# First layer's experts: state-space work queued behind the activation, the output gate folded into the last group, shorter root and norm chains

## The chip, the cores and the metric

The kernel runs on one core of a Trainium2 chip. The time is the device time of one execution in microseconds (us); less is better. For the kernel before there are three runs and one profiled execution, which is a run of its own.

## The reference, cut to what matters

A two-layer backbone over 512 tokens (256 of context, 256 latent) of width 1024. Every layer normalises the stream with a modulated RMSNorm, mixes, adds a gated residual, and then runs a mixture of experts over a second modulated norm. The first layer treats context and latent tokens alike in shape, but with modulation rows of their own (`cg2` and `g2` below); the second layer's experts see the latent tokens alone.

```python
f = hier_moe(jnp.concatenate([modnorm(xc, norm_g[i, 1], csh2, csc2),
                              modnorm(x, norm_g[i, 1], sh2, sc2)], axis=1), *moe_p)
xc = xc + cg2 * f[:, :n_ctx]
x = x + g2 * f[:, n_ctx:]
...
def rmsnorm(t, g):
    tf = t.astype(F32)
    y = tf * lax.rsqrt(jnp.mean(tf * tf, axis=-1, keepdims=True) + EPS)
    return (y * g.astype(F32)).astype(t.dtype)
...
hid = jax.nn.silu(t @ w_gate[e]) * (t @ w_up[e])
y = y + gates[:, e:e + 1] * (hid @ w_down[e])
```

There are 32 experts, each token goes to two of them. All arithmetic is float32.

## The kernel before, in words

The stream X stands in four tiles of 128 tokens by 1024 (tiles 0 and 1 context, 2 and 3 latent). In `tail` a layer's experts are worked off in groups: 13 in the first layer, 11 in the second. A group holds two or four experts that share the 128 rows of one tile of gathered tokens, 64 or 32 rows each. `pair` does one group:

- the gate and up products into one PSUM bank (tag g, L242), with weight tiles of 1 MB from a ring of buffers that SP loads in order (L1592);
- the next group's gathered rows are transposed on PE and copied (`pair_rows`, `then`);
- SiLU on ScalarE (L1748), the product with the up half on VectorE (L1749);
- two transposes of the hidden tile, a copy (`cp`, L254 on VectorE or L256 on ScalarE; without an engine's name the two take turns), and the down products into two banks (tag m);
- each half of y, times the token's gate, is split in a rounded part (ScalarE, L1772) and the rest (VectorE, L1773);
- a 0/1 matrix S takes the rows back to token order, tile by tile (tag c), and VectorE adds each 128x512 result to a sum F (L1786).

In the last group `add` takes the place of the sum in F: in the first layer it multiplies by the gate row and adds to X (L1553, L1554; three of the eight additions go to GpSimd). The sums F of the earlier groups are multiplied by the gate row and added to X by `gated` (L1542, L1543), two tiles before the last group's SiLU (`work`) and two behind its product L1749 (`after`). In the second layer's last group the gate row is already multiplied into the halves (`cols`, L1768 to L1770), and `add` is one addition (L1551).

Beside the first layer's groups 2 to 12 runs `s5_prepare`, a generator of 67 steps: small vector work, zeroing copies, two passes of products for the second layer's state-space operators (`prod`, L1147 to L1155), PE transposes and small products. `pair` calls it six steps at a time, `self.work(work)`, in front of SiLU.

The second layer begins with `norm1`: the squares of each tile on ScalarE (L436), a root for a pair of tiles on VectorE (`rsqrt_`, L174 to L185, ten dependent steps on a column or a few), the scaling of both tiles (L453, 128x1024 each), then transposes on PE (L246, four to a bank) and evictions with scale and shift (L469, L471). The first layer's `norm1`, near the start of the kernel, is the same with plain copies, and stands among the modulation products, whose weight tiles are loaded four ahead. `rsqrt_` also serves the tail's tiles (one column), the heads (ten columns), the filter (four) and the final norm (two).

The order of the instructions on each engine is fixed when the program is built: a scheduler takes the instructions in the order of writing, as they become ready by its own estimates. `issue_after(ins)` queues what its block writes for the engine of `ins` behind `ins`, on that engine alone. The lines are those of the profile.

Of the kernel before, what the change touches and what calls it, by code (L numbers as in the profile page):

```python
# [21 lines left out]
P = 128  # L22
# [8 lines left out]
SHARE = ((0, 0), (1, 0), (2, 0))  # L31
# [130 lines left out]

def small(pool, name, n):

    return pool.tile([P, 10], F32, name=name, tag=name)[:, :n]


def rsqrt_(nc, pool, src, n, scale, src2=None):


    V = nc.vector
    x, y, t, q = (small(pool, "rs" + c, n) for c in "xytq")
    if src2 is None:
        V.tensor_scalar(x, src, float(scale), EPS, op0=ALU.mult, op1=ALU.add)  # L174
    else:
        V.scalar_tensor_tensor(x, src, EPS, src2, op0=ALU.add, op1=ALU.add)
    V.tensor_scalar(y.bitcast(I32), x.bitcast(I32), -0.5, float(0x5F375C00), op0=ALU.mult, op1=ALU.add)
    V.scalar_tensor_tensor(t, y, -0.5, y, op0=ALU.mult, op1=ALU.mult)
    V.tensor_mul(t, t, x)
    V.scalar_tensor_tensor(y, t, 1.5009, y, op0=ALU.add, op1=ALU.mult)  # L180
    V.tensor_mul(t, y, y)
    V.tensor_mul(t, t, x)
    V.tensor_scalar(q, t, 0.375, -1.25, op0=ALU.mult, op1=ALU.add)
    V.tensor_mul(q, q, t)
    V.scalar_tensor_tensor(y, q, 1.875, y, op0=ALU.add, op1=ALU.mult)  # L185
    return y
# [44 lines left out]
class Body:  # L231
# [193 lines left out]
    def rms(self, tiles, tmp):  # L425

        n = len(tiles)
        if n == 1:
            ss = small(self.sm, "ss", 2)
            for h in range(2):  # L430
                cs = slice(512 * h, 512 * h + 512)
                self.nc.scalar.activation(tmp[0], self.X[tiles[0]][:, cs], AF.Square, scale=1.0 / 32, accum_out=ss[:, h:h + 1])
            return rsqrt_(self.nc, self.sm, ss[:, 0:1], 1, 1.0, ss[:, 1:2])
        ss = small(self.sm, "ss", n)
        for j, i in enumerate(tiles):
            self.nc.scalar.activation(tmp[j], self.X[i][:], AF.Square, accum_out=ss[:, j:j + 1])  # L436
        return rsqrt_(self.nc, self.sm, ss, n, 1.0 / D)

    def norm1(self, layer):
# [9 lines left out]
        for b in range(2):  # L449
            xn = [next(ring) for _ in range(2)]  # L450
            r = self.rms([2 * b, 2 * b + 1], xn)
            for i in range(2):
                nc.vector.tensor_scalar(xn[i], self.X[2 * b + i][:], r[:, i:i + 1], None, op0=ALU.mult)  # L453
            for j in range(4):
# [3 lines left out]
                for k in range(4):  # L458
                    d, i = 2 * j + k // 2, k % 2
                    self.tr(ps[:, 128 * k:128 * k + 128], xn[i][:, 128 * d:128 * d + 128])  # L460
# [895 lines left out]
    def tail(self, layer, tiles, mix, mixT):  # L1356
# [5 lines left out]
        with ExitStack() as es:  # L1362
# [164 lines left out]
            for q in range(nG):  # L1527
# [9 lines left out]
                gate2 = lambda t: row(g2, 0 if local else t // 2)  # L1537
                if q == nG - 1:
# [9 lines left out]
                    def add(n, cs, ps):  # L1548
                        t = tiles[n]
                        if local:  # L1550
                            V.tensor_add(self.X[t][:, cs], self.X[t][:, cs], ps)  # L1551
                            return
                        V.tensor_mul(F[n][:, cs], gate2(t)[:, cs], ps)  # L1553
                        (nc.gpsimd if (n, cs.start) in SHARE else V).tensor_add(self.X[t][:, cs], self.X[t][:, cs], F[n][:, cs])  # L1554
# [5 lines left out]
                               (row(g2, 0), row(g2, 1)) if local and final else None, q == 0 and not local)  # L1560
# [170 lines left out]
    def pair(self, q, xT, T, part, n, tokc, gate, F, work=0, after=0, then=None, cols=None, new=False):  # L1731
# [15 lines left out]
        self.work(work)  # L1747
        nc.scalar.activation(hid, ps[:, :256], AF.Silu)  # L1748
        m = V.tensor_mul(hid, hid, ps[:, 256:])  # L1749
        if after:  # L1750
            with self.tc.issue_after(m.ins):
                self.work(after)
# [3 lines left out]
        self.cp(hidT, ps[:, :256].rearrange("p (k t) -> p k t", t=128))  # L1756
# [49 lines left out]
    def final(self):  # L1806
# [4 lines left out]
        for t in (2, 3):  # L1811
            u = self.unit()
            y.append(u.f[:, :D])
            for h in range(2):
                nc.scalar.activation(u.f[:, D:D + 512], self.X[t][:, 512 * h:512 * h + 512], AF.Square, scale=1.0 / 32, accum_out=ss[:, k:k + 1])
                k += 1
# [226 lines left out]
```

## Time and profile before

| | us |
|---|---|
| median of 3 runs | 1200.01 (1198.22 to 1200.25) |
| the profiled execution's own time | 1194.71 |
| its span, first to last instruction | 1192.7 |
| PE busy | 1087.7 |
| VectorE busy | 699.0 |
| ScalarE busy | 319.2 |
| read from HBM and written | 298.82 MB, mean 251 GB/s |

Times in rows are in us from the span's start. PE is the matrix engine, PEld its weight loads, DVE is VectorE, ACT ScalarE, POOL GpSimd, SP the queue that issues most loads. A name such as psg is the PSUM tile of tag g. A group of rows gives busy time, count and mean; the chain of waits gives the pieces of work that the end depended on, in order of time. A matrix product of float32 is recorded as two PE instructions, a transpose as one.

### The profile page before, as it was taken

What the parts mean: (1) busy time and instruction counts of PE and PEld (TensorE: products, weight loads), DVE (VectorE), ACT (ScalarE), POOL (GpSimd) and SP (SyncE); (2) the same over time, 40 slices, a digit from 0 to 9 for tenths busy, and PEclk for the clock granted to TensorE, in tenths of its full rate; (3) what the DMA queues carried; (4) which work ended last, traced back from release to release, by engine and by line L of the source; (5) the groups of instructions that cost most, each with busy time, mean ns of one, the idle gap of its engine ahead of it and who ended that gap; (6) DMA issues with size and microseconds to landing.
All of it is one profiled execution on the core that took longest, in us unless ns stands there. A gap on an engine that the chain in (4) does not pass through costs nothing.

```text
span 1192.7 us, 17395 instructions
## 1 busy us (share of the span) xinstructions
PE 1087.7 (91%) x6528; PEld 560.3 (47%) x6528; DVE 699.0 (59%) x1915; ACT 319.2 (27%) x651; POOL 52.6 (4%) x64
## 2 busy tenths in 40 slices
PE   5999999999998899989989879999989899999975
PEld 2356556544456333334435246556665554444331
DVE  4876889558567375363453678857564554433324
ACT  3323212135123211120221065245442221212111
POOL 0001410000000100000000100010000000000000
PEclk9999999959999899999999889999989899999998
DMA  8777533640404589999798512345637285999994
GB/s 306 283 266 265 212 131 129 239 196 4 173 36 135 206 349 419 421 419 413 294 421 320 208 36 75 121 137 201 231 137 292 83 342 229 422 421 421 420 420 190
DMA packets 48601, 298.82 MB, mean 251 GB/s; under 512 B 6407, under 2 KB 8984, under 8 KB 15165
## 3 DMA queue, kind: packets, MB, share of 16 engines
q1 hardware_dynamic: 40380, 281.58, 60.4%
q10 hardware_dynamic: 5728, 11.86, 2.7%
q0 software_dynamic: 2400, 4.19, 1.0%
q8 instruction: 54, 0.88, 0.3%
q14 instruction: 39, 0.31, 0.1%
HBM read 295.68 MB, written 4.26 MB: 251 GB/s over the span
## 4 chain that ended last, share of the span: by engine, by line
PE 45%; DVE 10%; DMA 9%; ACT 2%; issue 1%; DVEq 0%; SPq 0%; ACTq 0%
PE psg L242 15%; PE psm L242 13%; PE psc L242 11%; DMA big<-w_e 9%; PE pst L242 3%; PE pst L246 2%; DVE big L1280 1%; PE psc L825 1%; DVE big L1216 1%; DVE big L1147 1%; DVE fr L1773 1%; ACT fr L1772 0%; DVE big L254 0%; ACT big L1155 0%; DVE big L1212 0%
## 5 line engine op out<-in xcount | busy, mean ns | idle before, releaser
L242 PE MATMUL psm<-big 128*128 128x512 f32 (+8 forms) x672 | 197.7, 466 | 4.6 <-ACT big L256 2.4
L242 PE MATMUL psg<-big,big 128*32 128x512 f32 (+1 forms) x720 | 176.6, 618 | 9.6 <-DMA big<-w_e 9.6
L242 PE MATMUL psm<-big,big 128*32 128x64 f32 (+7 forms) x600 | 129.2, 446 | 8.0 <-DVE big L254 4.1
L242 PEld LDWEIGHTS psm<-big 128*128 128x128 f32 (+2 forms) x672 | 91.3, 166 | 87.8 <-issue 64.7
L242 PE MATMUL psc<-big 128*32 128x32 f32 (+8 forms) x1108 | 111.6, 268 | 17.3 <-ACT big L514 7.8
L242 PE MATMUL psg<-big 128*64 128x512 f32 (+1 forms) x264 | 95.6, 617 | 8.1 <-PEq L1621 6.7
L242 PEld LDWEIGHTS psc<-big 128*32 128x32 f32 (+3 forms) x1108 | 73.7, 128 | 56.2 <-issue 29.7
L242 PE MATMUL psc<-fr 128*128 128x512 f32 x296 | 94.0, 431 | 4.1 <-DVE fr L1773 3.1
L1786 DVE TENSOR_TENSOR big<-big,psc 128x512 f32<-128x512 f32 x128 | 82.6, 684 | 22.0 <-PE psc L242 21.5
L246 PE MATMUL pst<-k_par,big 128*128 128x128 f32 (+2 forms) x470 | 80.5, 299 | 15.8 <-DVE big L453 3.7
L246 PEld LDWEIGHTS pst<-k_par,big 128*128 128x128 f32 (+2 forms) x470 | 55.8, 149 | 68.0 <-issue 30.1
L242 PEld LDWEIGHTS psc<-fr 128*128 128x128 f32 x296 | 49.5, 187 | 76.8 <-DVE big L1786 20.3
L242 PEld LDWEIGHTS psg<-big,big 128*32 128x32 f32 (+1 forms) x720 | 44.2, 124 | 86.2 <-issue 69.8
L242 PEld LDWEIGHTS psm<-big,big 128*32 128x32 f32 (+2 forms) x600 | 54.0, 145 | 51.8 <-issue 39.2
L1773 DVE SCALAR_TENSOR_TENSOR fr<-psm,tab,fr 128x512 fp32r<-128x512 f32 x46 | 34.6, 751 | 74.1 <-ACT fr L1772 71.7
L256 ACT ACTIVATE big<-pst 128x512 f32<-128x512 f32 (+2 forms) x88 | 47.3, 547 | 92.2 <-PE pst L246 85.0
L242 PE MATMUL psm<-parts 128*128 128x512 f32 x264 | 67.8, 405 | 0.5 <-DVE parts L651 0.5
L242 PE MATMUL psm<-big,bm 128*64 128x512 f32 (+1 forms) x256 | 56.4, 644 | 9.7 <-DVE bm L254 6.0
L242 PEld LDWEIGHTS psm<-parts 128*128 128x128 f32 x264 | 48.1, 188 | 19.0 <-issue 7.2
L1772 ACT ACTIVATE fr<-psm,tab 128x512 fp32r<-128x512 f32 x46 | 31.6, 687 | 70.9 <-PE psm L242 70.9
L242 PEld LDWEIGHTS psg<-big 128*64 128x64 f32 (+1 forms) x264 | 25.1, 131 | 48.5 <-issue 45.7
L1749 DVE TENSOR_TENSOR big<-big,psg 128x256 f32<-128x256 f32 x11 | 4.6, 420 | 72.3 <-ACT big L1748 72.3
(399 smaller groups left out, 1379.5 us busy)
## 6 DMA issues: line engine op xcount, KB each, us to landing
big<-w_e SPq DMA_DIRECT2D x187, 1024.0 KB, 15.8
big<-w_mod SPq DMA_DIRECT2D x36, 1024.0 KB, 5.1
x<-w_mod SPq DMA_DIRECT2D x12, 1024.0 KB, 4.9
big<-w_out SPq DMA_DIRECT2D x8, 1024.0 KB, 6.7
big<-w_hy SPq DMA_DIRECT2D x6, 1024.0 KB, 6.0
big<-modd ACTq DMA_DIRECT2D x10, 512.0 KB, 10.9
x<-w_e SPq DMA_DIRECT2D x5, 1024.0 KB, 13.6
h2d<-big ACTq DMA_DIRECT2D x6, 512.0 KB, 4.5
```

What stands on the lines that cost most here:

```text
L242: self.product = self.nc.tensor.matmul(out, lhsT, rhs, start=start, stop=stop)
L246: return self.nc.tensor.transpose(out, in_, self.ident[:k, :k])
L256: self.nc.scalar.activation(out, in_, AF.Copy)
L825: m = self.nc.tensor.matmul(ps[:, :k.shape[-1]], q, k, start=True, stop=True)
L1147: V.tensor_mul(sc[:, j, :].rearrange("p (d u v h) -> p d u v h", d=2, u=4, v=4), tab(x), bc_(c + y, perm))
L1216: V.scalar_tensor_tensor(v, self.iota[:, :128], self.s5l[:, ix(y):ix(y) + 1], v, op0=ALU.mult, op1=ALU.add)
L1280: V.tensor_tensor_scan(z, R[:, 16 * d + 4 * qq + q:16 * d + 4 * qq + q + 1].to_broadcast([P, 128]), z, 0.0, op0=ALU.mult, op1=ALU.add)
L1749: m = V.tensor_mul(hid, hid, ps[:, 256:])
L1772: nc.scalar.activation(hi, pd[hf][:], AF.Copy, scale=gate)
L1773: V.scalar_tensor_tensor(lo, pd[hf][:], gate, hi.bitcast(F32), op0=ALU.mult, op1=ALU.subtract)
L1786: V.tensor_add(F[t][:, cs], F[t][:, cs], ps[:])
```

## The change

Five things are edited.

1. `rsqrt_` works with a halved and rescaled argument, so that a step is left out; for one or two columns a square and its product with the argument are one instruction per column.
2. `norm1` no longer scales the tiles. It scales a 128x128 identity by the root (`dg`), and PE multiplies X itself by it, in place of the transpose.
3. In the first layer, the group before the last builds one gate row per token row: `gs` is the context's row or the latent's, as the token number says. The last group multiplies it into the halves of y by `cols`, as the second layer does, and `add` is a single addition in both layers. No addition goes to GpSimd.
4. In `pair`, the work beside a group of the first layer is written behind the product L1749, in `issue_after`, in place of in front of SiLU. The last group keeps its two pieces.
5. Where a group has such work, the hidden copy goes to ScalarE.

```diff
 def rsqrt_(nc, pool, src, n, scale, src2=None):
...
+    def square():
+        for j in [slice(j, j + 1) for j in range(n)] if n <= 2 else ():
+            V.scalar_tensor_tensor(t[:, j], y[:, j], x[:, j], y[:, j], op0=ALU.mult, op1=ALU.mult)
+        if n > 2:
+            V.tensor_mul(t, y, y)
+            V.tensor_mul(t, t, x)
...
-    V.scalar_tensor_tensor(t, y, -0.5, y, op0=ALU.mult, op1=ALU.mult)
-    V.tensor_mul(t, t, x)
-    V.scalar_tensor_tensor(y, t, 1.5009, y, op0=ALU.add, op1=ALU.mult)
-    V.tensor_mul(t, y, y)
-    V.tensor_mul(t, t, x)
-    V.tensor_scalar(q, t, 0.375, -1.25, op0=ALU.mult, op1=ALU.add)
-    V.tensor_mul(q, q, t)
-    V.scalar_tensor_tensor(y, q, 1.875, y, op0=ALU.add, op1=ALU.mult)
+    V.tensor_scalar(y.bitcast(I32), x.bitcast(I32), -0.5, MAGIC, op0=ALU.mult, op1=ALU.add)
+    square()
+    V.scalar_tensor_tensor(y, t, -1.5009, y, op0=ALU.add, op1=ALU.mult)
+    square()
+    V.scalar_tensor_tensor(q, t, -5.0 / 3, t, op0=ALU.add, op1=ALU.mult)
+    V.scalar_tensor_tensor(y, q, 1.25, y, op0=ALU.add, op1=ALU.mult)
...
+            dg = [x[:, :P] for x in xn]
             for i in range(2):
-                nc.vector.tensor_scalar(xn[i], self.X[2 * b + i][:], r[:, i:i + 1], None, op0=ALU.mult)
+                nc.vector.tensor_scalar(dg[i], self.ident[:], r[:, i:i + 1], None, op0=ALU.mult)
...
-                    self.tr(ps[:, 128 * k:128 * k + 128], xn[i][:, 128 * d:128 * d + 128])
+                    self.mm(ps[:, 128 * k:128 * k + 128], self.X[2 * b + i][:, 128 * d:128 * d + 128], dg[i], True, True)
...
+                if q == nG - 2 and not local:
+
+                    gs, m = row(xgu[0], nG % 2), small(self.sm, "branch", 2)
+                    for b, op in enumerate((ALU.is_le, ALU.is_gt)):
+                        V.tensor_scalar(m[:, b:b + 1], self.entry(nG - 1)[0], 256.0, None, op0=op)
+                    nc.scalar.activation(gs, row(g2, 0), AF.Copy, scale=m[:, 0:1])
+                    V.scalar_tensor_tensor(gs, row(g2, 1), m[:, 1:2], gs, op0=ALU.mult, op1=ALU.add)
...
-                        if local:
-                            V.tensor_add(self.X[t][:, cs], self.X[t][:, cs], ps)
-                            return
-                        V.tensor_mul(F[n][:, cs], gate2(t)[:, cs], ps)
-                        (nc.gpsimd if (n, cs.start) in SHARE else V).tensor_add(self.X[t][:, cs], self.X[t][:, cs], F[n][:, cs])
+                        V.tensor_add(self.X[t][:, cs], self.X[t][:, cs], ps)
...
-                               (row(g2, 0), row(g2, 1)) if local and final else None, q == 0 and not local)
+                               None if not final else (row(g2, 0), row(g2, 1)) if local else (gs, row(xgu[0], (nG - 1) % 2)), q == 0 and not local)
...
-        self.work(work)
+        if after:
+            self.work(work)
         nc.scalar.activation(hid, ps[:, :256], AF.Silu)
         m = V.tensor_mul(hid, hid, ps[:, 256:])
-        if after:
-            with self.tc.issue_after(m.ins):
-                self.work(after)
+        with self.tc.issue_after(m.ins):
+            self.work(after or work)
...
-        self.cp(hidT, ps[:, :256].rearrange("p (k t) -> p k t", t=128))
+        self.cp(hidT, ps[:, :256].rearrange("p (k t) -> p k t", t=128), "s" if after or work else None)
```

The squares of the tails and of the final norm take the new scale with them (`math.sqrt(HALF) / 32`).

## Rows read from the trace of the kernel before

**Rows 1.** The page, busy time and share of the span of each engine.

```profile
PE 1087.7 (91%) x6528; PEld 560.3 (47%) x6528; DVE 699.0 (59%) x1915; ACT 319.2 (27%) x651; POOL 52.6 (4%) x64
```

**Rows 2.** Busy time by stretch: length, then PE, PEld, DVE, ACT, POOL, PEclk, DMA share, GB/s.

```profile
572.00:600.00 28.00, 25.32 (x206) 11.68 (x204) 15.99 (x27) 6.47 (x12) 0.99 (x1) 0.98 0.76 286
600.00:641.00 41.00, 40.26 (x269) 18.16 (x262) 16.11 (x27) 6.38 (x11) 0.00 (x0) 0.97 1.01 420
1010.00:1095.00 85.00, 82.81 (x518) 37.05 (x511) 32.96 (x81) 15.29 (x31) 0.00 (x0) 1.00 1.01 421
```

**Rows 3.** The chain of waits in the second group: start, length, what.

```profile
422.88 1.02 PE pst L246 x8
...
424.29 0.39 ACT bm L256
...
424.73 3.65 PE psm L242 x16
```

**Rows 4.** The pauses of groups 7 and 10 by stretch; the S5 products, 500 to 610.

```profile
524.38:528.21 3.83, 1.46 (x11) 0.98 (x11) 3.24 (x6) 2.69 (x6) 1.46 (x1) 1.00 1.01 419
594.99:599.10 4.11, 1.43 (x10) 0.98 (x10) 3.78 (x8) 2.74 (x6) 0.99 (x1) 0.96 1.01 427
...
L1155 ACT ACTIVATE big<-big 64x512 f32<-64x512 f32 x16 | 9.8, 625 | 21.6 <-DVE big L1149 20.6 <-DVE big L1151 0.9
L1147 DVE TENSOR_TENSOR big<-s5Wp,big 128x512 f32<-128x512 f32 x8 | 5.2, 687 | 2.7 <-PE psg L242 2.6
```

**Rows 5.** The chain of waits in the last group of the first layer.

```profile
666.71 0.39 ACT bm L1748
...
667.54 2.27 DVE big L1542 x2
669.81 2.27 DVE x L1543 x2
...
672.47 6.04 PE psm L242 x16
```

**Rows 6.** Timeline of ACT and DVE: a plain group's end, then the last group's.

```profile
531.11 0.69 ACT L1772 ACTIVATE fr<-psm,tab 128x512 fp32r<-128x512 f32 x1 [2.44 <-PE psm L242]
...
538.95 0.69 DVE L1786 TENSOR_TENSOR big<-big,psc 128x512 f32<-128x512 f32 x1 [0.70 <-PE psc L242]
...
689.26 0.69 DVE L1554 TENSOR_TENSOR x<-x,big 128x512 f32<-128x512 f32 x1
```

**Rows 7.** Timeline of the second layer's last group.

```profile
1178.18 1.61 DVE L1768 SCALAR_TENSOR_TENSOR big<-psm,tab,big 128x512 f32<-128x512 f32 x2 [3.97 <-PE psm L242]
1179.03 0.63 ACT L1769 ACTIVATE fr<-big 128x512 fp32r<-128x512 f32 x1 [7.87 <-DVE big L1768]
```

**Rows 8.** The chain of waits in the second layer's norm, and PE's timeline there.

```profile
691.72 1.40 DVE big L453 x2
...
694.41 0.17 DVE rsy L185
...
698.29 1.97 PE L246 MATMUL pst<-k_par,big 128*128 128x128 f32 x8 [0.38 <-DVE big L471]
```

**Rows 9.** The chain in the second layer's experts: gathering products, plain float32.

```profile
955.64 3.78 PE pst L242 x32
```

**Rows 10.** Timeline of PE and SP at the start of the kernel.

```profile
16.22 1.94 PE L246 MATMUL pst<-k_par,big 128*128 128x128 f32 x8 [3.12 <-DVE big L510]
...
27.80 3.64 PE L242 MATMUL psg<-big,cT 128*32 128x512 f32 x16
...
29.79 8.54 SPq L300 DMA_DIRECT2D big<-w_mod  x4
```

**Rows 11.** Timeline at the end: the last step of the final root.

```profile
1186.68 0.16 DVE L185 SCALAR_TENSOR_TENSOR rsy<-rsq,rsy 128x2 f32<-128x2 f32 x1
```

More of the change, by code (lines that the diff above doesn't have):

```diff
@@ L30 @@
 EARLY = (4, 4)
-SHARE = ((0, 0), (1, 0), (2, 0))
 SPLIT = lambda nc: nc.vector
@@ L160, in layout_inputs @@
     return o
+HALF, MAGIC = 0.5 / 2.25, -554172480.0
 def small(pool, name, n):
@@ L172, in rsqrt_ @@
     x, y, t, q = (small(pool, "rs" + c, n) for c in "xytq")
+    def square():
[4 more added lines that the diff above has]
+            V.tensor_mul(t, t, x)
     if src2 is None:
-        V.tensor_scalar(x, src, float(scale), EPS, op0=ALU.mult, op1=ALU.add)
+        V.tensor_scalar(x, src, float(scale * HALF), EPS * HALF, op0=ALU.mult, op1=ALU.add)
     else:
-        V.scalar_tensor_tensor(x, src, EPS, src2, op0=ALU.add, op1=ALU.add)
-    V.tensor_scalar(y.bitcast(I32), x.bitcast(I32), -0.5, float(0x5F375C00), op0=ALU.mult, op1=ALU.add)
-    V.scalar_tensor_tensor(t, y, -0.5, y, op0=ALU.mult, op1=ALU.mult)
-    V.tensor_mul(t, t, x)
-    V.scalar_tensor_tensor(y, t, 1.5009, y, op0=ALU.add, op1=ALU.mult)
-    V.tensor_mul(t, y, y)
-    V.tensor_mul(t, t, x)
-    V.tensor_scalar(q, t, 0.375, -1.25, op0=ALU.mult, op1=ALU.add)
-    V.tensor_mul(q, q, t)
-    V.scalar_tensor_tensor(y, q, 1.875, y, op0=ALU.add, op1=ALU.mult)
+        V.scalar_tensor_tensor(x, src, EPS * HALF, src2, op0=ALU.add, op1=ALU.add)
+    V.tensor_scalar(y.bitcast(I32), x.bitcast(I32), -0.5, MAGIC, op0=ALU.mult, op1=ALU.add)
[4 more added lines that the diff above has]
+    V.scalar_tensor_tensor(y, q, 1.25, y, op0=ALU.add, op1=ALU.mult)
     return y
@@ L431, in rms @@
                 cs = slice(512 * h, 512 * h + 512)
-                self.nc.scalar.activation(tmp[0], self.X[tiles[0]][:, cs], AF.Square, scale=1.0 / 32, accum_out=ss[:, h:h + 1])
+                self.nc.scalar.activation(tmp[0], self.X[tiles[0]][:, cs], AF.Square, scale=math.sqrt(HALF) / 32, accum_out=ss[:, h:h + 1])
             return rsqrt_(self.nc, self.sm, ss[:, 0:1], 1, 1.0, ss[:, 1:2])
@@ L1814, in final @@
             for h in range(2):
-                nc.scalar.activation(u.f[:, D:D + 512], self.X[t][:, 512 * h:512 * h + 512], AF.Square, scale=1.0 / 32, accum_out=ss[:, k:k + 1])
+                nc.scalar.activation(u.f[:, D:D + 512], self.X[t][:, 512 * h:512 * h + 512], AF.Square, scale=math.sqrt(HALF) / 32, accum_out=ss[:, k:k + 1])
                 k += 1
```

## The prediction

> **What bounds the kernel now.** I read the page's busy times first: PE is busy for nine tenths of the span [rows 1], so a gain has to be a pause of PE, or work of PE. The table by stage says where that holds. In the first layer's experts the weight stream and PE take turns: at 572 to 600 us the DMA engines are only three quarters busy, because PE has not yet given buffers back, and at 600 to 641 both are full [rows 2]. From 1010 us to the end of the second layer's experts the stream runs at 421 GB/s without a break [rows 2]; there the stream's start decides, and whatever moves that start moves the end by as much. So an earlier end of the first layer passes to the end of the kernel, unless a stage between absorbs it; from 700 to 945 us I found no wait for a weight load on the chain, and I let the shift pass in full.
>
> Next the chain of waits, group by group. In a plain group (the second) PE finishes gate and up at 422.88, does the next group's eight transposes, and starts the down products at 424.73: 1.85 us, with the hidden copy on ScalarE at 0.39 us [rows 3]. Two later groups pause for longer: 3.83 and 4.11 us, with DVE busy for 3.24 and 3.78 of it [rows 4]. There the second layer's S5 products (L1147 to L1155) stand in front of the group's own product L1749. The last group is the worst: gate and up end at 666.7, and the down products start at 672.47, 5.8 us later, because the two tiles of gated sums (4.54 us) sit between L1749 and the hidden copy on VectorE [rows 5].
>
> **The change, part by part.** Four parts.
>
> *The last group's copy on ScalarE.* ScalarE does nothing between that group's SiLU and the down products. With the copy there the pause is the plain one, 1.85 us [rows 3]: the products start at 668.5, 4.0 us earlier. They take 6.04 us now [rows 5]; the same 16 take 3.65 us in the plain group [rows 3], behind a short pause. I take 3.65, so they end at 672.2, not 678.5: 6.3 us. The gated sums run on under them and end at 672.1, just before VectorE is wanted; if they ended later, each us would count.
>
> *The gate folded into the last group.* Now every sum is a product with the gate row and an addition, the last ending at 689.95, 11.4 us after the down products [rows 5, 6]. Afterwards there is one addition per sum, as in any plain group, where the last ends 8.5 us after them (531.1 to 539.64) [rows 6]. The halves are built in one step more, as in the second layer's last group: a product of some 0.8 us, then a copy of 0.63 us in place of 0.69 [rows 7]. So some 9.3 us: the last sum ends at 681.5, 8.4 us earlier. The merged gate row (one 1024-wide copy on ScalarE, one product on VectorE, two tiny comparisons, no DMA) goes into the group before; VectorE is busy for 16 of 41 us there [rows 2], which hides it; without that cover it costs 1.3 us, by the 1024-wide operations of rows 5 (2.27 us for two). GpSimd loses three sums; it queues nothing else that anybody waits for.
>
> *Norm of the second layer, and the roots.* From the last sum to the second pair's first transpose is 8.3 us now (689.95 to 698.29) [rows 6, 8]. In it lie ten dependent steps of a root, the first pair's two scalings in the middle (1.40 us), and the second pair's own. A root for two columns becomes nine steps, two pairs of which overlap: some 0.4 us less. A scaling becomes 128 columns in place of 1024; I estimate 0.2 us in place of 0.70. Together, some 3 us less, and the evictions L471 wait less behind the scalings. Against it stand the products. A transpose is one PE instruction, eight in 1.02 us [rows 3], 0.128 us each; a plain fp32 product of that size is two, thirty-two instructions in 3.78 us [rows 9], 0.236 us for a product. Sixteen in the second pair cost 1.7 us more at full rate. At the half rate (1.2 GHz in place of 2.4) eight transposes took 1.97 us [rows 8], and the sixteen would cost 3.6 us more. Net −2 us, between −5 (the rate stays full, and the evictions flow) and +2 (half rate, and the first pair's doubled products hold up the second). The Trainium skill (TensorE: Matmul & The Clock Gate, section Terms) calls the transpose mode four times faster for FP32, which speaks against this part; by it the sixteen would cost 6.1 us more and the part would lose. The trace has both forms and shows 1.8 times, so I go by the trace.
> Elsewhere a root for one column loses three of ten steps of 0.2 us: 0.6 us at the last tile before each layer's experts, where the routing waits for it, and 0.4 us at the end, where the output waits for the last step at 1186.68 [rows 11]. Sum −1.6 us; the other roots lie beside PE work, which is the cover; without it they gain some 2 us more.
>
> *Start of the kernel.* The same exchange in the first layer's norm falls on a busy PE at the lower rate: eight transposes take 1.94 us, and behind them in PE's queue stand the modulation products (3.64 us, from 27.80), whose buffers SP waits for to load the other four weight tiles, 8.54 us of issuing [rows 10]. Sixteen products in place of transposes add 3.9 us ahead of that point, and sixteen behind it 1.7. VectorE gives back some 1.1 us twice, as by the scalings of rows 8. Should PE reach the full rate earlier, the 3.64 us halve and the addition vanishes. Bounds: −2 and +5; I take +2, nearer to the rows than to the hope.
>
> *The S5 work behind the activation.* The six steps per group are now queued on VectorE behind L1749. It moves VectorE's share alone; its ScalarE copies, its two kinds of DMA on ScalarE's queue and its PE products follow as they become ready. Gain at most: the two long pauses back to plain, 2.0 + 2.3 us [rows 3, 4], less what the weights allow. Cost: behind L1749 now stand some five products before the low half of y, which VectorE has to make about 6 us after gate and up end (1.85 + 3.65 + 0.69). Half a product pass is four multiplications and two sums of 0.69 us at most, 4.1 us after the hidden product and one row copy (1.5 us): it just fits. The four ScalarE copies of 0.63 us [rows 4] may stand ahead of the high half, 1.3 us at four groups. SP gets no new issue, but a scratch unit may come free later and hold its queue by one load, 2.5 us (1 MB at 420 GB/s) [rows 2]. So between −4.2 and +5; I take −1.5. The earlier groups gain nothing, since the stream paces them. The row copies, which changed places each group, now keep theirs: the form of rows 3, at no cost.
>
> **The sum.** −8.4 −2 −1.6 +2 −1.5 = −11.5 us. Against the profiled execution's own time of 1194.71 (span 1192.7) that is 1183.2. The median of the runs is 1200.01, 5.3 us above that execution, so I forecast 1188.5 for the median.
>
> **The rivals.**
> *Work in the way of y (slower).* The moved work takes the place of the wait removed: VectorE and ScalarE reach the halves of y and the sums late, and PE waits there. The two product passes are 9.8 us of ScalarE copies and, on VectorE, 16 multiplications (5.2 us for eight) and eight sums like them [rows 4], some 25 us. It turns the sign once over 13 us of it land on PE's path. With three quarters, 19 us, in place of the −1.5: 1209. For it: nothing else holds VectorE back after L1749. Against: four such groups only, and by the sum above each fits between the hidden product and y, if by 0.6 us only. 0.07.
> *A product as dear as four transposes (slower).* X as the stationary operand could load worse than the gathered rows of rows 9. At four times 0.128 us the 64 products of both norms cost 24.6 us more than the transposes, not 6.9, and if PE is the bound of both norms the time is 17.7 us longer, 1206. Rows 3 and 9 speak against it: 1.8 times. 0.02. (The factor is that of the Trainium skill, TensorE: Matmul & The Clock Gate, section Terms.)
> *PE at the half rate, fillers in the gap.* The hand-over keeps its earlier start, but the second layer's modulation products, which are queued to fill PE there, stand between the sums and the doubled products, and both norms run at the low rate: 2 us lost in the fold, +2 in place of −2, +3 in place of +2 at the start, 1195.5. For it: the lower clock today in exactly these places [rows 8, 10]. 0.18.
> *The change does not do what it says at the last group.* Were the copy still late (another ScalarE copy first), 6.3 us would be lost: 1194.8. Nothing in the trace stands on ScalarE there. 0.06.
> *The parts cancel.* Start at +5, pauses unchanged, norm at +2: 1198 to 1202. 0.05.
>
> **How the numbers follow.** The forecast as told has 0.62; its own range is 1180 to 1194. The range of 8 in 10 takes in the cancelled gains and the bounds downwards: 1178 to 1198. A measurement of this kernel can tell about 0.2%, 2.4 us. Faster by more: the forecast and the two rivals at 1195, 0.86; the same: 0.05; slower: 0.07 + 0.02 = 0.09.
>
> **What would show it.** In the changed profile: the last group's hidden copy on ScalarE and its down products within 2 us of gate and up, which take some 3.7 us; one addition per sum, the last some 9 us after them; in groups seven and ten no L1147 ahead of the product, and a pause under 2 us; 32 products of two instructions in place of 32 transposes in each norm; at the start, modulation products before or after 27.8 us. It is wrong if PE waits for the halves of y in groups seven to eleven, if the down products stay at 6 us, or if the stream in the second layer starts no earlier though the first layer ends earlier.

## The result and the profile after

| | before | changed |
|---|---|---|
| median of runs, us | 1199.12 (1193.04 to 1200.25, 4 runs) | 1180.22 (1175.89 to 1182.28, 4 runs) |
| ratio | | 0.9853, 95% interval 0.9828 to 0.9877 |
| the profiled execution: own time, span | 1194.71, 1192.7 | 1179.0, 1176.9 |

The change makes the kernel 1.5% faster. The forecast was 1188.5 in a range of 1178 to 1198: the direction and the range held, and the gain is larger than forecast (15.8 us between the spans of the two profiled executions, 18.9 us between the medians, against 11.5).

The page of the changed kernel, its busy times. PE has 64 instructions more than before [rows 1] and is busy for 10 us less; its mean granted clock is 0.968 where it was 0.963.

```profile
PE 1077.5 (92%) x6592; PEld 565.0 (48%) x6592; DVE 688.9 (59%) x1875; ACT 322.6 (27%) x659; POOL 48.0 (4%) x61
```

The last group of the first layer, changed kernel, PE's timeline. Gate and up end at 663.74; the down products follow 1.9 us later, against 5.8 [rows 5], and the sixteen take 3.66 us, against 6.04.

```profile
662.72 1.02 PE L249 MATMUL psg<-big,big 128*64 128x512 f32 x2
664.67 0.44 PE L253 MATMUL psg<-k_par,bm 128*128 128x128 f32 x2 [0.93 <-DVE bm L1761]
665.64 3.66 PE L249 MATMUL psm<-big,bm 128*64 128x512 f32 x16 [0.53 <-ACT bm L263]
...
680.37 2.02 PE L249 MATMUL pst<-big,x 128*128 128x128 f32 x16 [0.98 <-DVE big L461]
682.74 2.05 PE L249 MATMUL pst<-big,x 128*128 128x128 f32 x16 [0.34 <-DVE big L479]
685.13 2.05 PE L249 MATMUL pst<-big,x 128*128 128x128 f32 x16 [0.34 <-DVE big L479]
...
687.91 1.95 PE L249 MATMUL pst<-big,x 128*128 128x128 f32 x16
```

The last four lines are the second layer's norm: 64 instructions where there were 32 transposes, 2.05 us for sixteen at the full rate. VectorE's timeline of the same stretch has one addition per sum; the last ends at 678.26, before it was 689.95 [rows 6]:

```profile
671.84 0.69 DVE L1565 TENSOR_TENSOR x<-x,psc 128x512 f32<-128x512 f32 x1
...
677.57 0.69 DVE L1565 TENSOR_TENSOR x<-x,psc 128x512 f32<-128x512 f32 x1 [0.68 <-PE psc L249]
```

Busy times by stretch there (pause, down products, sums, norm): PE's granted clock is at the full 2.4 GHz (1.00) throughout.

```profile
663.70:665.60 1.90, 0.48 (x3) 0.20 (x2) 1.41 (x2) 0.77 (x2) 0.00 (x0) 1.00 1.02 431
665.60:669.30 3.70, 3.66 (x20) 1.18 (x24) 3.70 (x5) 0.00 (x0) 0.00 (x0) 1.00 0.99 419
669.30:678.30 9.00, 8.49 (x41) 3.35 (x44) 7.64 (x14) 4.72 (x9) 1.72 (x3) 1.00 0.45 157
678.30:691.10 12.80, 11.13 (x82) 8.62 (x75) 7.84 (x33) 6.31 (x13) 0.00 (x0) 1.00 0.26 83
```

In the kernel before, the same four stretches had 0.83, 0.60, 1.00 and 0.75; the second and the fourth of them:

```profile
672.50:678.50 6.00, 6.00 (x17) 1.66 (x17) 0.08 (x1) 0.69 (x1) 0.00 (x0) 0.60 0.18 75
690.00:703.90 13.90, 8.89 (x38) 6.15 (x39) 9.56 (x33) 6.09 (x13) 0.00 (x0) 0.75 0.23 77
```

The down products took 6 us there because PE had stood nearly idle for 5.8 us and ran them mostly at 1.2 GHz.

The pauses between gate and up and the down products, read off PE's timeline for each of the 13 groups:

| group | 1 | 2 | 3 | 4 | 5 | 6 | 7 | 8 | 9 | 10 | 11 | 12 | 13 |
|---|---|---|---|---|---|---|---|---|---|---|---|---|---|
| before | 3.50 | 1.85 | 1.99 | 1.84 | 1.89 | 1.84 | 3.83 | 2.40 | 6.00 | 4.11 | 2.11 | 3.95 | 5.80 |
| changed | 3.50 | 1.84 | 1.97 | 1.85 | 1.91 | 1.94 | 1.90 | 2.72 | 8.73 | 1.93 | 3.08 | 8.73 | 1.90 |

Groups 7 and 10 are plain now [rows 4]. Groups 9 and 12 have grown: S5's PE transposes and small products now stand in one block before the down products (567 to 574 us, and 637 to 644), where PE is busy with them. Group 11's pause is 1.2 us longer than the 1.90 that it has in the two runs without the merged gate row (u_fold and u_last below): the row's 1024-wide copy stands on ScalarE in front of the hidden copy. The next SiLU comes no later for it (20.8 us after group 11's, 20.7 and 20.8 in those runs).

```profile
615.91 1.14 ACT L1551 ACTIVATE big<-big,branch 128x1024 f32<-128x1024 f32 x1
```

The moved work also made a wait that was not there. In group 3 VectorE does some fifty small S5 operations between the hidden product (442.75) and the low half of y, changed kernel, VectorE and then PE:

```profile
442.75 0.42 DVE L1761 TENSOR_TENSOR bm<-bm,psg 128x256 f32<-128x256 f32 x1 [3.51 <-ACT bm L1760]
443.09 0.18 DVE L1070 SCALAR_TENSOR_TENSOR big<-big 128x32 f32<-128x32 f32 x1
...
450.97 0.25 DVE L1098 TENSOR_TENSOR big<-big 128x96 f32<-128x96 f32 x1
451.14 1.40 DVE L1784 SCALAR_TENSOR_TENSOR fr<-psm,tab,fr 128x512 fp32r<-128x512 f32 x2
```

```profile
451.94 1.83 PE L249 MATMUL psc<-fr 128*128 128x512 f32 x4 [2.45 <-DVE fr L1784]
453.70 1.97 PE L249 MATMUL psg<-big 128*64 128x512 f32 x2
```

PE waits 2.45 us, and the products behind run at the half rate (2 in 1.97 us, against 1.02). Group 4's SiLU comes 23.7 us after group 3's, against 18.9 before. By group 7 nothing of this is left: from group 1's to group 7's SiLU it is 120.9 us, against 123.4 before. The place where it is given back is group 6: its down products wait for a weight load in the kernels with the old order (8.3 us for all of them before, 8.4 in u_order below), and in the changed kernel the load is there in time (4.7 us). u_order, then the changed kernel:

```profile
511.09 3.62 PE L249 MATMUL psm<-big,bm 128*32 128x512 f32 x20 [0.84 <-DMA big<-w_e]
```

```profile
506.10 4.68 PE L249 MATMUL psm<-big,bm 128*32 128x512 f32 x32 [0.53 <-ACT bm L263]
```

### The profile page after: what moved, and what is told of

Read it like the earlier page. It is cut to its first block, busy times and chain, and to the rows that moved or that the text cites. A ratio compares the mean times of both kernels' runs of the same rounds, so it can differ in the third digit from the quotient of the medians.

```text
span 1176.9 us, 17482 instructions
## 1 busy us (share of the span) xinstructions
PE 1077.5 (92%) x6592; PEld 565.0 (48%) x6592; DVE 688.9 (59%) x1875; ACT 322.6 (27%) x659; POOL 48.0 (4%) x61
## 5 line engine op out<-in xcount | busy, mean ns | idle before, releaser
L249 PE MATMUL psm<-big 128*128 128x512 f32 (+8 forms) x672 | 194.4, 462 | 4.6 <-ACT big L263 2.4
L249 PE MATMUL psg<-big,big 128*32 128x512 f32 (+1 forms) x720 | 171.8, 605 | 10.1 <-PEq L1632 6.0
L253 PE MATMUL pst<-k_par,big 128*128 128x128 f32 (+1 forms) x406 | 67.5, 290 | 7.2 <-DVE big L261 1.9
L253 PEld LDWEIGHTS pst<-k_par,big 128*128 128x128 f32 (+1 forms) x406 | 46.1, 143 | 50.3 <-issue 28.4
L249 PE MATMUL psm<-big,bm 128*64 128x512 f32 (+1 forms) x256 | 51.0, 597 | 5.9 <-ACT bm L263 5.3
L1760 ACT ACTIVATE bm<-psg 128x256 f32<-128x256 f32 x13 | 5.0, 385 | 156.8 <-PE psg L249 156.8
L1761 DVE TENSOR_TENSOR bm<-bm,psg 128x256 f32<-128x256 f32 x13 | 5.5, 422 | 69.9 <-ACT bm L1760 69.9
## 6 DMA issues: line engine op xcount, KB each, us to landing
big<-modd ACTq DMA_DIRECT2D x10, 512.0 KB, 10.6
```

The source lines that it names most:

```text
L249: self.product = self.nc.tensor.matmul(out, lhsT, rhs, start=start, stop=stop)
L253: return self.nc.tensor.transpose(out, in_, self.ident[:k, :k])
```

## The experiments

Beside the runs of the result, the runs came in three sets, each on one chip with runs of the kernel before next to them. The runs of one kernel differ by up to 18 us, more than any part is worth, so each experiment is read in its trace as well, by five stretches: **A** to the first SiLU of the first layer's experts, **B** from that to the last group's SiLU, **C** to the last sum, **D** to the last eviction of the second layer's norm, **E** the rest. GB/s is the rate from 1030 to 1090 us.

| kernel | A | B | C | D | E | GB/s | span | median | ratio to before (95%) |
|---|---|---|---|---|---|---|---|---|---|
| before | 402.1 | 264.6 | 23.2 | 13.9 | 488.9 | 421 | 1192.7 | | |
| changed | 403.2 | 260.6 | 14.5 | 12.8 | 485.9 | 426 | 1176.9 | 1180.22 | 0.9853 (0.9828 to 0.9877) |
| same_again | 400.7 | 261.2 | 14.5 | 12.8 | 485.5 | 426 | 1174.6 | 1179.20 | 0.9846 (0.9797 to 0.9894) |
| u_order | 406.4 | 263.1 | 14.8 | 13.9 | 485.7 | 426 | 1184.0 | 1184.69 | 0.9884 (0.9845 to 0.9923) |
| u_copy | 399.5 | 261.0 | 20.1 | 12.8 | 486.9 | 426 | 1180.3 | 1189.21 | 0.9928 (0.9900 to 0.9957) |
| u_fold | 412.4 | 262.9 | 17.1 | 14.8 | 488.0 | 420 | 1195.2 | 1187.66 | 0.9927 (0.9901 to 0.9953) |
| u_norm2 | 402.4 | 261.8 | 14.5 | 13.5 | 487.5 | 426 | 1179.6 | 1183.87 | 0.9891 (0.9859 to 0.9923) |
| u_norm1 | 403.2 | 260.6 | 14.5 | 12.8 | 487.5 | 426 | 1178.5 | 1182.18 | 0.9862 (0.9805 to 0.9919) |
| u_roots | 407.9 | 260.7 | 14.5 | 13.0 | 486.3 | 426 | 1182.4 | 1186.23 | 0.9898 (0.9841 to 0.9955) |
| c_mix | 407.8 | 259.6 | 14.5 | 12.8 | 487.0 | 426 | 1181.7 | 1179.78 | 0.9839 (0.9790 to 0.9887) |
| b_last | 403.3 | 264.9 | 14.8 | 12.3 | 485.9 | 427 | 1181.2 | 1182.72 | 0.9891 (0.9851 to 0.9931) |
| u_last | 400.1 | 263.1 | 23.9 | 14.0 | 489.4 | 420 | 1190.5 | 1193.10 | 0.9969 (0.9943 to 0.9994) |
| d_12 | 403.5 | 261.2 | 14.8 | 14.0 | 487.0 | 426 | 1180.5 | 1181.98 | 0.9878 (0.9838 to 0.9918) |
| c_mix8 | 408.1 | 262.6 | 14.8 | 13.9 | 488.8 | 426 | 1188.2 | 1187.93 | 0.9921 (0.9892 to 0.9950) |

### The changed kernel once more (same_again)

> The changed kernel itself once more, as the measure for the runs beside it. Theory A (its parts gain in every execution): the same stages as in its first trace, 14.5 us from the last group's SiLU to the last sum, 12.8 us from there to the last eviction of the norm, a ratio of about 0.985. Theory B (part of the gain was the execution's luck with the stream's rate and the clock): these two stages agree, but the first SiLU and the length of the second layer's stream move by some us between executions, and the ratio moves towards 0.988 to 0.99.

B to D repeat within 0.6 us, C and D within 0.02. A moves by 2.5 us, but the ratio is the same (0.9846): theory A for the ratio and the stages; of theory B only the moving A was seen. Differences of C and D by a few tenths can thus be read from one trace, differences of A cannot.

### The hidden copy on VectorE again (u_copy)

```diff
-        self.cp(hidT, ..., "s" if after or work else None)
+        self.cp(hidT, ..., "v" if after else "s" if work else None)
```

> The changed kernel with the last group's hidden copy on VectorE again, everything else as changed. Theory A (the prediction's term): the copy waits for the two tiles of gated sums again, the down products start 4 us later and take 6.0 in place of 3.7 us, and the end comes 6.3 us later. Theory B: the start alone counts, since the modulation products that PE puts between keep it at the full rate: 4 us later. Theory C: the fold has taken the last sums off VectorE, so the late start is hidden behind the additions: under 1.5 us later.

C is 5.7 us longer, and the time is 9 us above the changed kernel's (0.0075, with intervals of 0.003 each, so that the 5.7 us lie within what the times allow). The stretches of this kernel (from gate and up to the hidden transposes, the wait, the down products):

```profile
659.50:661.80 2.30, 1.37 (x6) 0.31 (x3) 0.86 (x2) 0.38 (x1) 0.00 (x0) 1.00 1.02 431
661.80:666.20 4.40, 0.06 (x1) 0.00 (x0) 4.40 (x5) 0.00 (x0) 0.00 (x0) 0.74 1.00 422
666.20:672.10 5.90, 5.81 (x17) 1.62 (x17) 0.79 (x2) 0.00 (x0) 0.00 (x0) 0.61 0.17 70
```

PE is idle for 4.4 us, VectorE full with the gated sums, and the sixteen products behind run at a mean clock of 0.61: 5.86 us. From SiLU to the first product it is 5.76 us against 1.86, so 3.9 us of start and 2.2 of rate. Theory A; B lacks the rate, and C's hiding is not there.

### The fold undone (u_fold)

```diff
-                if q == nG - 2 and not local:
...
-                        V.tensor_add(self.X[t][:, cs], self.X[t][:, cs], ps)
...
+                        V.tensor_mul(F[n][:, cs], gate2(t)[:, cs], ps)
+                        (nc.gpsimd if (n, cs.start) in SHARE else V).tensor_add(self.X[t][:, cs], self.X[t][:, cs], F[n][:, cs])
...
```

> The changed kernel with the gate row multiplied to every sum of the last group again (eight products, three of the eight additions on GpSimd), with the early copy, norm and roots as changed. Theory A (the prediction's terms): the last sum comes 11.4 us after the down products in place of 9.3, so 2.1 us later. Theory B: with the products 4 us earlier the gated sums of the second half of the tiles and the products of the sums meet on VectorE, which becomes the bound: 3.5 us or more later. Theory C: the step that the fold adds to the halves of y costs as much as it saves: within 0.7 us of the changed kernel.

C is 2.6 us longer, near theory A's 2.1. But the norm behind it is 2.1 us longer too, which no theory had. Its stretches (sums, wait, norm):

```profile
679.90:691.40 11.50, 11.49 (x54) 3.61 (x48) 9.66 (x15) 4.59 (x7) 6.37 (x6) 1.00 0.42 152
691.40:694.00 2.60, 0.00 (x0) 0.00 (x0) 2.42 (x16) 1.38 (x4) 0.00 (x0) 0.90 0.00 0
694.00:703.20 9.20, 8.87 (x49) 8.55 (x50) 4.61 (x18) 2.82 (x5) 0.00 (x0) 0.66 0.14 30
```

PE has nothing to run for 2.6 us behind the sums, and the doubled products then run at a clock of 0.66. So the fold gives 4.6 us up to the norm's end, 2.1 of them through the norm's rate. The stream is slower here too, of which more below.

### The last group alone undone, and alone made (u_last, b_last)

The first is the changed kernel with the two edits above; the second the kernel before with the fold and, in the last group of each layer, the copy on ScalarE.

> The last group alone undone: hidden copy on VectorE and a product per sum, with the new order, norms and roots. Theory A (the parts add): 23.2 us from the last group's SiLU to the last sum, norm 12.8 as in the changed kernel, 8.7 us slower than that. Theory B (behind the long sums PE stands idle, the granted clock falls, and the norm's doubled products run at the half rate): the norm takes 14.8 us or more, as in the run with the fold undone, 10.7 us or more slower in all. Theory C: the norm is shorter than 12.8 us, since the first pair of tiles is long done.

> The last group alone changed: the copy on ScalarE and the gate folded in; S5 order, both norms, roots and the other copies as in the kernel before. Theory A (the parts add): the way from the last group's SiLU to the last sum is 14.5 us in place of 23.2, the norm behind it 13.9 as before, and the time is 8 to 9.5 us below the kernel before (a ratio of about 0.9925). Theory B (the earlier sums also keep the clock of the old norm up): the norm takes 13.2 us or less as well, 9.5 us or more in all. Theory C (a later stage absorbs part of it): under 6 us.

Without the last group's edits the change is worth 0.3% (0.9969): C is 23.9 us, D 14.0, together 10.6 us more than in the changed kernel. The clock is 0.83 in the 4 us ahead of the norm and 0.91 in it, so theory B's mechanism is there at a smaller size, and the 10.6 us lie between A (8.7) and B's bound (10.7). With them alone it is worth 1.1% (0.9891), 13 us of 1196: C is 8.4 us shorter, D 1.6 although this is the old norm, and E 3.0. Theory B of the second. The two ratios add up to about the whole (0.3 and 1.1 against 1.5): the last group is most of the change.

### The second layer's norm as before (u_norm2)

```diff
+            old = layer == 1
             for i in range(2):
...
+                if old:
+                    nc.vector.tensor_scalar(xn[i], self.X[2 * b + i][:], r[:, i:i + 1], None, op0=ALU.mult)
...
+                    if old:
+                        self.tr(ps[:, 128 * k:128 * k + 128], xn[i][:, 128 * d:128 * d + 128])
...
```

> The changed kernel with the second layer's norm as before (both tiles scaled by VectorE, transposes on PE); the first layer's norm, the roots and the rest as changed. Theory A (the prediction's term): 2 us later. Theory B (the trace after the change, where the way from the last sum to the last eviction is 1.1 us shorter than before, 0.2 of it the root): 0.9 us later. Theory C (PE at the full rate is what bounds the changed norm, 2.05 us for a bank of sixteen instructions against 1.02 us for eight transposes): the old form is as fast or faster, 0 to 2 us below the changed kernel.

D is 0.7 us longer, near theory B's number. Yet with the old S5 order it is the other way: C and D of b_last (old norm and root) are 27.1 us, of u_order (new ones) 28.8. So the new norm wins 0.7 us in one setting and loses 1.7 in another, and no gain of its own is shown. Two things set the sign. In u_norm2 PE stands idle in front of and between the first transposes (1.35, 0.22 and 0.91 us), and the next two sets of eight run at a granted clock of 0.55 and take 1.97 us each; in b_last, where a burst of modulation products stands between, the clock stays at 1.00, eight take 1.11, and the old norm's D of 12.25 us is shorter than the new one's 12.77. So the 0.7 us go with the clock, and at the full rate, by this one trace, theory C holds; the changed kernel with the old norm at the full rate was not seen. u_norm2, then b_last:

```profile
683.58 1.97 PE L253 MATMUL pst<-k_par,big 128*128 128x128 f32 x8 [0.91 <-DVE big L486]
```

```profile
688.89 1.11 PE L249 MATMUL pst<-k_par,big 128*128 128x128 f32 x8 [0.92 <-DVE big L482]
```

And in u_order a modulation burst stands between the doubled products (PE's timeline):

```profile
686.45 1.35 PE L249 MATMUL pst<-big,x 128*128 128x128 f32 x10 [1.25 <-DVE big L461]
687.73 1.07 PE L249 MATMUL psg<-big,cT 128*32 128x512 f32 x8
688.73 1.83 PE L249 MATMUL pst<-big,x 128*128 128x128 f32 x14
```

### The first layer's norm as before (u_norm1)

The same edit, for the first layer alone.

> The changed kernel with the first layer's norm as before (scaled tiles, transposes), the second layer's as changed. Theory A (the prediction's term): the first mixer products start 2 us earlier, and so does the end. Theory B (the trace after the change, where they start 0.4 us later than before): 0.4 us earlier, within what can be told, since the doubled products bring PE to its full rate by 23 us in place of 32 and the modulation products then take 1.9 in place of 3.6 us. Theory C: without the products the rate comes late and the start is later than in the changed kernel.

The first mixer products start at 51.5 us. Over all traces the old form gives 52.4, 52.1 and 51.5, the new one 52.4 to 55.7 with a median of 53.2 (eleven): 1 us later, between theories A and B, and lost in the spread of A. In the changed kernel the second sixteen instructions of the first pair already run at the full rate, and the modulation burst behind them takes 1.90 us, where it took 3.64 [rows 10]; it holds ten instructions in place of sixteen, but with the next burst it is eighteen in both, in 2.96 us against 4.69:

```profile
18.28 3.78 PE L249 MATMUL pst<-big,x 128*128 128x128 f32 x16
...
23.11 2.05 PE L249 MATMUL pst<-big,x 128*128 128x128 f32 x16
...
27.00 1.90 PE L249 MATMUL psg<-big,cT 128*32 128x512 f32 x10
```

### The longer roots (u_roots)

> The changed kernel with the longer root everywhere (ten dependent steps). Theory A (the prediction's term): 1.6 us later: 0.6 at the last tile before each layer's experts and 0.4 at the end; the way from the last sum to the norm's last eviction grows by 0.4 to 0.8. Theory B (from the trace after the change, where nine steps of 0.2 us follow each other and the two column steps do not overlap): 0.2 us in the norm, 0.2 at the end, and the routing's roots lie beside other work: 0.5 us or less in all.

D is 0.2 us longer, and from the second layer's last SiLU to the end it takes 0.2 us more (23.25 against 23.0 to 23.1). The way from the norm to the second layer's first SiLU is 0.5 us longer (251.6 against 251.1), but that is the clock: a burst of 154 small products at about 840 us takes 7.7 us here and 6.2 in the trace of the changed kernel. Among the traces with the slow burst, the three with the longer root (before, b_last, u_roots) take 251.1 to 251.6 us on this way, those with the shorter one 252.4 to 252.7 (six) and 254.1 (c_mix8): there the shorter roots lose about 1 us. Most of it (0.8 to 1.1, beside c_mix) is there by 110 us behind the norm, on the stretch where the heads' roots (ten columns) stand; why stays open. So 0.4 us are gained, about 1 is lost, and theory A falls. What the root before the first layer's experts is worth stays open, since A moved by 4.7 us for another reason. Two column steps hold up the chain as long as the two steps that they replace (0.38 us to the next step); the changed kernel's chain at the end, and [rows 8] for the old steps of 0.17:

```profile
1169.70 0.18 DVE rsy L187
1169.91 0.36 DVE rst L179 x2
1170.29 0.17 DVE rsy L189
1170.49 0.36 DVE rst L179 x2
```

### The S5 work in front of SiLU again (u_order)

```diff
-        if after:
-            self.work(work)
+        self.work(work)
...
-        with self.tc.issue_after(m.ins):
-            self.work(after or work)
+        if after:
+            with self.tc.issue_after(m.ins):
+                self.work(after)
```

> The changed kernel with the S5 steps of groups 2 to 12 written in front of SiLU again; copies, fold, norm and roots stay as changed. Theory A (the prediction's term): the order alone gains 1.5 us, so this comes out 1.5 us above the changed kernel, with a bound of 4.2: the pauses of groups 7 and 10 return to about 3.9 us. Theory B (from the trace after the change): the order lost 4.8 us at group 3, where the small vector steps stand between the hidden product and the low half of y, and the stream gave it back by group 7, so group 3's SiLU comes 4 to 5 us earlier here while the last group's SiLU and the time stay within 1 us of the changed kernel. Theory C (work in the way of y costs at the end too): 2 us or more below the changed kernel.

Both A and B in part. The pauses of groups 7 and 10 return (3.28 and 4.12 us), and group 3 to 4 is 19.0 us again, 4.7 less. The last SiLU comes 1.9 to 2.5 us later after the first than in the two traces of the changed kernel, so the order gains 2 us or so; with the slower stream (before against u_fold and u_last) it is 1.6, the copies of the other groups included. Theory C fell.

### Twice as much work behind each activation (d_12)

`BG = (1, 12)` in place of `(1, 6)`.

> The changed kernel with twelve S5 steps behind each group's activation in place of six, so that six groups carry what twelve did. Theory A (the rival of the prediction, work in the way of y): the halves of y of four or five groups come 4 to 8 us late, PE waits for them, and the last group's SiLU comes 10 us or more later. Theory B (the stream gives it back): single groups are late by that much, yet the last group's SiLU is within 3 us of the changed kernel. Theory C (the last groups gain more, being plain again, with the stream full to the end): 2 to 4 us earlier.

The rival of the prediction, made as bad as it gets. The SiLUs of groups 5 to 8, and the last, in this kernel:

```profile
482.95 0.39 ACT L1760 ACTIVATE bm<-psg 128x256 f32<-128x256 f32 x1 [11.90 <-PE psg L249]
514.77 0.39 ACT L1760 ACTIVATE bm<-psg 128x256 f32<-128x256 f32 x1 [7.81 <-PE psg L249]
540.63 0.39 ACT L1760 ACTIVATE bm<-psg 128x256 f32<-128x256 f32 x1 [13.39 <-PE psg L249]
567.88 0.39 ACT L1760 ACTIVATE bm<-psg 128x256 f32<-128x256 f32 x1 [12.23 <-PE psg L249]
...
664.70 0.38 ACT L1760 ACTIVATE bm<-psg 128x256 f32<-128x256 f32 x1 [12.20 <-PE psg L249]
```

In the changed kernel those are 484.72, 504.23, 524.09, 544.30 and 663.78. Group 8 is 23 us late, and the last group 0.6 (B: 261.2 us). Theory B in its numbers, though not only for its reason: later groups, rid of S5 work, are shorter (18.5 us from group 12's SiLU to group 13's, where it was 28.2). C and D are 1.5 us longer, with the same gap between the norm's first products as in u_order.

### Two versions that might beat both (c_mix, c_mix8)

```diff
-        if after:
+        ahead = after or self.bg is not None and not hasattr(self, 'ops')
+        if ahead:
             self.work(work)
...
-            self.work(after or work)
+            self.work(after if ahead else work)
```

The second takes eight steps per group as well.

> The changed kernel with the S5 steps of groups 2 to 7 (small vector work and zeroing copies) in front of SiLU, and those from the first product pass on behind the hidden product as changed. Theory A (the stream paces the early groups): group 3's SiLU comes 4.8 us earlier after the first group's (from 23.7 to 19.0 us behind group 2), the lead is gone by group 7, and the last group's SiLU and the time are within 1 us of the changed kernel. Theory B (what group 3 loses is kept to the end): 2 to 4 us faster than the changed kernel. Theory C (the order behind the activation helps the early groups too): 1 to 2 us slower.

> Eight S5 steps per group in place of six, those before the first product pass in front of SiLU and the rest behind the hidden product. Theory A: the S5 products leave the last two groups, PE no longer stands between the stream and its buffers there (it moved 262 GB/s in the stretch before the last SiLU), and from the first to the last SiLU it takes 257 us in place of 261: 2 to 4 us faster than the changed kernel. Theory B (the same PE work stands elsewhere, and PE is busy 95% of this stage anyway): 259 to 261 us, no difference that can be told.

c_mix frees group 3 (18.9 us to the next) and has the shortest B, 259.6, by 1.0 to 1.6 us; the time (0.9839 against 0.9846 beside it) shows no difference: theory A in the time, at or past its bound of 1 us in B. c_mix8 keeps the lost time elsewhere: group 7 to group 10 takes 81.0 us in place of 69.9, group 12 to 13 9.7 less (18.5), and B is 262.6. Theory A fell; B's bound was missed by 1.6 us. Its time is worse than the changed kernel's (0.9921, interval 0.9892 to 0.9950, against 0.9828 to 0.9877). No version beats the changed kernel measurably.

## Why the prediction was right, step by step

The forecast and the measured terms, by the stretches of the two profiled executions:

| stretch | forecast | measured |
|---|---|---|
| A: start, one root | +1.4 | +1.1 |
| B: S5 order | -1.5 | -4.0 |
| C: copy and fold | -8.4 | -8.8 |
| D: norm and its roots | -2 | -1.1 |
| E: two roots | -1.0 | -3.0 |
| sum | -11.5 | -15.8 |

C is the one row in which the forecast's mechanism and its size both hold. A's +1.1 says little, since A moves by 2.5 us when the same kernel runs twice. The measured median of 1180.2 lies near the lower end of the range, in part because of gains in B and E that were not forecast; that much is luck.

**The copy on ScalarE** (forecast 6.3 at the products): 3.9 us of start and 2.2 of rate, 5.7 at the last sum. Taking 3.65 us for the sixteen products, by the plain group, was the right choice; the cause of the old 6.04 is the clock behind the pause.

**The fold** (2.1 on top): 2.6, and with it 2.1 us of the norm's rate, which I had put into a rival as a loss of both together. The hand-over passed on as forecast: the second layer's first SiLU is 13.1 us earlier, 12.8 of it there already at the norm's end. So "a stage between absorbs it" did not happen. The merged gate row was hidden, but not by VectorE, as forecast: its copy on ScalarE lengthens group 11's pause by 1.2 us, and the group's end does not show it.

**The second layer's norm** (-2, of it 0.4 the root): mis-sized. Its price was right: sixteen instructions take 2.05 us, eight transposes 1.02 to 1.11, a factor of about two. The Trainium skill (TensorE: Matmul & The Clock Gate, section Terms) calls the transpose mode four times faster for FP32; no trace here shows that factor. The gain was not right: the scaling leaves VectorE's path, but PE is then busy for 11.1 of the 12.8 us, and its filling products come between. The old form was priced at the half rate that it had; once the last group hands over early, it can keep the full rate as well (b_last: 12.25 us, against 13.86 before and 12.77 changed). The runs show 0.7 gained to 1.7 lost, so the -1.1 of D is not the new norm's.

**The roots** (-1.6): "two pairs of which overlap" failed; a pair of column steps holds the chain for 0.38 us, as the two steps did that it replaces. Shown are 0.2 us in the norm and 0.2 at the end, and against them about 1 us lost between the second layer's norm and its experts.

**The start** (+2): 1 us in the median. The way out that the prediction named, an earlier full rate, sped up the modulation products as it said (4.69 to 2.96 us) and took back part of the price.

**The S5 order** (-1.5): about -2, but not by the path forecast alone. The two pauses went as forecast. "It just fits by 0.6 us" was right for VectorE in the product groups: in group 7 it is done with its S5 products in time and then waits for the high half. That half, behind ScalarE's row copies, makes PE wait 1.42, 0.45 and 1.06 us in groups 7, 8 and 10 (forecast: 1.3 at four groups). So a sign that the prediction named for being wrong, PE waiting for the halves of y in groups seven to eleven, came about at the size that its own cost allows, and does not tell the two apart. PE's wait in group 7:

```profile
531.88 0.50 PE L249 MATMUL psc<-fr 128*128 128x512 f32 x1 [1.42 <-ACT fr L1783]
```

The larger wait came at group 3, where small steps, which the forecast had not counted, took 8 us of VectorE. "The earlier groups gain nothing, since the stream paces them" is why that cost nothing at the end: they lost 4.8 and had it back by group 7. In d_12 23 us are given back as well, there by later groups that have no S5 work left. The rival of work in the way of y fell on this, not on the small amount of work. Its 13 us for turning the sign are loose: the other terms add up to -10.0, so 10 us would do.

**The copies of the other groups** (nothing, "the form of rows 3, at no cost"): u_order and b_last have the same order, fold and stream rate, and within B they differ in these copies alone; B is 263.1 and 264.9 us. That is 1.8 us by one trace each, where traces of one order lie 1.2 apart; no run tested it alone.

**What was not forecast**: in the profiled execution the stream is faster (426 against 421 GB/s). Behind the second layer's first SiLU E is 2.7 us shorter, 0.2 of it the last root, and the stream paces this part. With the new order it is some 2 us of B as well (262.9 and 263.1 in the two traces at 420, 261.0 in the mean of six at 426); with the old order and copies it is nothing (264.6 at 421, 264.9 in b_last at 427), so how B's 4.0 us divide between order, copies and stream is not settled. Up to that SiLU E is 0.3 us shorter: the burst at about 840 us ran 1.5 us faster, which hides what the roots lose. That, the better order and the weaker norm and roots make up the difference to the forecast.

## What to carry to other kernels

Price a pause of PE with what runs behind it: 4 us of waiting cost 6 here, since the next sixteen products ran mostly at half the clock. Where a stream of weights paces a stage, a late group need not cost anything at the stage's end (4.8 us at group 3 were gone by group 7), so look for edits at the hand-over, where nothing follows to give the time back. Compare two forms of an operation at the clock that each will have after the change, not at the one it has now. When runs differ by more than the parts are worth, cut the trace into stretches and compare those.

## What the hardware showed that was not expected

**The time before the experts moves with the clock.** A ranges from 399.5 to 412.4 us, though the code of the mixer is the same. From 250 to 300 us PE is busy for over 47 of the 50 us in every trace, but its granted clock is not the same. The slowest and a fast one (u_fold, then same_again):

```profile
250.00:300.00 50.00, 49.64 (x158) 20.74 (x158) 26.74 (x93) 17.78 (x54) 0.00 (x0) 0.63 0.09 38
```

```profile
250.00:300.00 50.00, 48.01 (x215) 22.45 (x214) 37.19 (x121) 25.12 (x72) 0.00 (x0) 0.94 0.19 73
```

Their first SiLUs are at 412.4 and 400.7. In between lie 0.76 (407.9, u_roots), 0.82 (406.4, u_order) and 0.85 (403.2, changed). The order is not strict: 0.83 goes with 407.8 in c_mix. A second such place is the burst at 837 to 855 us: its 154 products take 6.22 us in four traces and 7.6 to 7.7 in ten; over the burst the granted clock is 1.00 in the changed kernel and 0.78 in u_norm1 and in the kernel before. The changed kernel, then u_norm1:

```profile
838.62 6.22 PE L249 MATMUL psm<-big,big 128*32 128x64 f32 x154 [0.82 <-DVE big L1297]
```

```profile
838.61 7.71 PE L249 MATMUL psm<-big,big 128*32 128x64 f32 x154 [0.81 <-DVE big L1304]
```

What sets the clock from one execution to the next was not found. The spread of the runs goes with it: of the 51 runs of the kernel before in the three sets, the five slowest (1206.2 to 1208.9 us) have a mean granted clock of 0.948 to 0.955, the five fastest (1190.8 to 1193.6) 0.961 to 0.967.

**The stream's rate goes with the fold.** All eleven traces with the fold show 426 or 427 GB/s, and the three without it (before, u_fold, u_last) 420 or 421, also side by side on one chip: u_fold, then u_copy.

```profile
1030.00:1090.00 60.00, 58.27 (x346) 26.02 (x338) 25.14 (x64) 11.89 (x24) 0.00 (x0) 1.00 1.01 420
```

```profile
1030.00:1090.00 60.00, 58.28 (x360) 26.18 (x358) 24.78 (x61) 11.43 (x23) 0.00 (x0) 1.00 1.01 426
```

The DMA engines are full in both. The difference is there hundreds of us away from the edited instructions (420 against 427 GB/s at 460 to 500 us, before and changed), so it is not what those do at that time. What in the program makes it stays open.
